# Values of the tile two back ahead of the transposes of the tile one back, in both attentions of an encoder layer

## The chip, the cores and the metric

The kernel runs on one core of one Trainium2 chip. The metric is the device time of one execution in microseconds (us); the time before is the median of three runs. A profile of one further execution shows what each engine did and when.

The engines have the names of the profile: PE is TensorE (matmuls; PEld is its loading of weights), DVE is VectorE, ACT is ScalarE, POOL is GpSimd, SP is the queue that issues most of the DMAs. PE writes only to PSUM, which has eight banks of 128 x 512 fp32 here; DVE and ACT read PSUM and copy to SBUF. Each engine works through its own queue in order.

## The reference

One encoder layer on two sequences (1024 and 256 rows of 1024 channels): a norm, one input projection, two attentions side by side, their gated sum, an output projection, and an MLP.

```python
def _layer(x, ...):
    h = _rmsnorm(x, g_mix)
    z = h @ w_in                       # qa, ka, va | qb, kb, vb | two gates
    gates = sigmoid(z[..., o6:] + b_gate)
    o_a, _ = _banded_attention(qa, ka, va, A_WINDOW, 1, rel_bias[:, :A_HEADS], sink)
    o_b = _dilated_mixture(qb, kb, vb, rel_bias[:, A_HEADS:])
    merged = gates[:, :, 0] * (o_a @ w_branch_a) + gates[:, :, 1] * (o_b @ w_branch_b)
    x = x + merged @ w_out
    h = _rmsnorm(x, g_mlp)
    return x + jnp.square(jax.nn.relu(h @ w_up)) @ w_down
```

Attention a has 8 heads in a window of 128 with a sink term in the denominator. Attention b has 12 heads in three groups of four, with dilations 1, 4 and 16; the three groups' outputs are merged by the softmax of their log-sums. In both, for a tile of 128 queries: scores = q k, plus a relative bias, minus the row maximum, exponential, row sum, and probabilities times values, divided by the sum.

## The kernel before

**Attention of one tile, in three steps.** Both attentions treat a tile of 128 queries and two heads at a time.

- scores: per head, PE multiplies q by k into a PSUM bank "sc" (two banks); DVE adds the bias and takes the row maximum in one instruction (L518 in attention b, L1027 in a), then negates the maxima (L521, L1031); ACT takes the exponential with the row sum (L523, L1033).
- transposes: PE turns the 128 x 128 blocks of probabilities (L534, L1048) into a bank "pt" (two banks, four blocks each), and copy() moves them to SBUF as the tile pt. A tile of b has two or four blocks, one of a four or six, so that six blocks need two banks.
- values: PE multiplies pt by v into the one bank "pv" (L546, L1062), copy() moves the result to SBUF as o, and POOL's queue stores o to DRAM.

copy() (L262, L264) gives its work to ACT and DVE in turn, in the order in which the program is written: the first call goes to ACT, the second to DVE, and so on.

**Attention b** runs beside the last five pairs of the input projection (about 355 to 590 us). All engines issue there in the order in which the program is written. attention_b() is a generator with three steps per tile, in the order scores(j), transposes(j - 1), values_of(j - 2) with load_v(j + 1). The projection calls tick() eighteen times per pair of columns, after each half of a group of matmuls (6 matmuls of 512 columns, or 12 of 256), and tick() takes two or three of these steps at a time: so many that the 188 steps are spread evenly over the calls. Between the calls stand the projection's own instructions: ACT copies or splits (a split is a copy rounded to the high part on ACT, "whi", and the subtraction of it on DVE, "wlo", L309 and L311), DVE sums, and once per pair four subtractions of 128 x 512 on POOL (L384 to L387), which combine the next pair's weights.

**Attention a** (about 598 to 755 us) has 40 tiles: 4 pairs of heads by 10 tiles of rows. A loop of 42 rounds runs, in round i, scores of tile i, transposes of tile i - 1 and values of tile i - 2. Between the steps tick(n) takes chunks of eight matmuls of logits() (five remaining gate columns, 31 chunks spread over 120 calls) and steps of the merge of attention b's groups. Up to round 35 a planner orders the instructions: it takes, for each engine, the earliest written instruction that it reckons to be ready. From round 36 on, through the sums of the sink and the division (sums_a, divide), the order of every engine is again that of the program. In rounds 36 to 39 turn_merged(i - 36) transposes the merged output of b into a bank "pt", ACT makes its high part, and low_b(i - 36) makes the low part on DVE, which frees the bank.

**The weights of what follows.** prepare() splits the next entry of a list of weights: five gate columns, then two pieces of w_branch_b, then four of w_branch_a, and so on. If its raw data has not been fetched, prepare() issues the load itself. weight(ahead) hands out the next entry, and splits entries until `ahead` more than that are ready: one more within logits(), none in the branches. Two raw loads, for the two pieces of w_branch_b, are issued at tick 96 and tick 104.

```python
def prepare(shared=False):
    i = len(ready)
    while len(raws) <= i:
        fetch()
    ...
def weight(ahead=None):
    i = taken[0]
    taken[0] += 1
    while len(ready) < min(len(specs), i + 1 + (AHEAD if ahead is None else ahead)):
        prepare()
    return ready[i]
```

**Behind the loop** sums_a() adds the sink to the denominators (DVE, an exponential on ACT, DVE), divide(t) divides the rows of attention a, open_gate() takes the sigmoids on ACT, the rest of the logits runs, and then the branches' products start, the first of them beside turn_a(0), which transposes the divided rows (L1194).

Of the kernel before, what the change touches and what calls it, by code (L numbers as in the profile page):

```python
# [97 lines left out]
def encoder_kernel(  # L98
# [125 lines left out]
# [5 lines that stand above are left out]
        _, shape, make = specs[i]  # L229
        hi, lo = make("whi", shape, F32R), make("wlo", shape, F32R)  # L230
        nc.scalar.activation(hi, raws[i], AF.Copy)
        h = shape[1] // 2 if shared else shape[1]
        for eng, k in ((nc.vector, slice(0, h)), (nc.gpsimd, slice(h, shape[1]))):
            if k.start < k.stop:
                eng.tensor_tensor(lo[:, k], raws[i][:, k], hi[:, k].bitcast(F32), op=ALU.subtract)
        ready.append((hi, lo))
# [240 lines left out]
    def attention_b(make):  # L477

        order = [(g, i, t, tile) for i in range(2) for g in (2, 1, 0) for t, tile in enumerate(_group_tiles(g))]
        n = len(order)  # L480
        held, live, bias = {}, {}, {}

        def load(j):

            if j >= n:
                return
            g, i, t, (pieces, W, _) = order[j]
            qk = held[j] = [make("qk", (P, 3 * P), n=3), None]
            for a, (p0, m, qa, ka) in enumerate(pieces):
                nc.sync.dma_start(qk[0][:, p0 : p0 + m], scr_qb[g][i][:, qa : qa + m])  # L490
                nc.sync.dma_start(qk[0][:, P + P * a : P + P * a + W], scr_kb[g][i][:, ka : ka + W])
            if t == 0:
                bias[g, i] = load_bias_b(g, i, make)

        def load_v(j):
            if j >= n:
                return
            g, i, t, (pieces, W, _) = order[j]
            v = held[j][1] = make("v", (P, 2, P), n=4)
            for a, (_, _, _, ka) in enumerate(pieces):  # L500
                for k in range(W // P):
                    nc.sync.dma_start(v[:, a + k, :], values_rows(g, i, ka // P + k))

        def scores(j):
            g, i, t, (pieces, W, c0) = order[j]
            qk, _ = held[j]
            whole, *flat = bias[g, i]
            b = whole[:, :, c0 : c0 + W] if c0 is not None else flat[pieces[0][2] >= NS]
            s = make("s", (P, 2, 2 * P), n=2)
            m = small.tile([P, 2], F32, name="m", tag="m")  # L510
            o = make("o", (P, ROW), n=6)
            for h in range(2):
                ps = bank("sc")
                rows = HALVES[h]
                for a, (p0, nq, _, _) in enumerate(pieces):
                    nc.tensor.matmul(ps[p0 : p0 + nq, :W], qk[rows, p0 : p0 + nq],
                                     qk[rows, P + P * a : P + P * a + W], start=True, stop=True)
                nc.vector.tensor_tensor_reduce(s[:, h, :W], ps[:, :W], b[:, h, :], 1.0, -3.0e38,  # L518
                                               op0=ALU.add, op1=ALU.max, accum_out=m[:, h : h + 1])
            nm, l = o[:, 2 * HD : 2 * HD + 2], o[:, 2 * HD + 2 :]  # L520
            nc.vector.tensor_scalar(nm, m, -1.0, None, op0=ALU.mult)  # L521
            for h in range(2):
                nc.scalar.activation(s[:, h, :W], s[:, h, :W], AF.Exp, bias=nm[:, h : h + 1],  # L523
                                     accum_out=l[:, h : h + 1])
            live[j] = s, o

        def transposes(j):
            W = order[j][3][1]
            s, o = live[j]
            pt = make("pt", (P, 4, P), n=2)  # L530
            ps = bank("pt")
            jobs = [(k, h) for k in range(W // P) for h in range(2)]
            for a, (k, h) in enumerate(jobs):
                nc.tensor.transpose(ps[:, P * a : P * a + P], s[:, h, P * k : P * k + P], ident)  # L534
            a = len(jobs)
            copy(pt[:, :a, :], ps[:, : P * a].rearrange("p (i q) -> p i q", q=P))
            live[j] = pt, o

        def values_of(j):
            g, i, t, (pieces, W, _) = order[j]  # L540
            (pt, o), (_, v) = live.pop(j), held.pop(j)
            pv = bank("pv")
            for h in range(2):
                for a, (p0, nq, _, _) in enumerate(pieces):
                    for k in range(W // P):
                        nc.tensor.matmul(pv[p0 : p0 + nq, HD * h : HD * h + HD], pt[:, 2 * k + h, p0 : p0 + nq],  # L546
                                         v[:, a + k, HALVES[h]], start=k == 0, stop=k == W // P - 1)
            copy(o[:, : 2 * HD], pv[:, : 2 * HD])
            for p0, nq, qa, _ in pieces:
                nc.gpsimd.dma_start(scr_b[g][qa : qa + nq, i, :], o[p0 : p0 + nq, :])  # L550

        load(0)
        load_v(0)
        yield
        load(1)
        yield
        for j in range(n + 2):
            if j < n:
                load(j + 2)
                scores(j)  # L560
            yield
            if 0 <= j - 1 < n:
                transposes(j - 1)
            yield
            if 0 <= j - 2 < n:
                values_of(j - 2)
            load_v(j + 1)
            yield

    def entering():  # L570
# [431 lines left out]
    if True:  # L1002
# [35 lines left out]
        def transposes(u, t):  # L1038
            W = tiles[t][1]
            s = live[u, t]  # L1040
            pt = a3("pt", (P, 6, P), 2)
            jobs = [(b, h) for b in range(W // P) for h in range(2)]
            banks = []
            for i, (b, h) in enumerate(jobs):
                if i % 4 == 0:
                    banks.append((i, min(len(jobs), i + 4), bank("pt")))
                ps = banks[-1][2]
                nc.tensor.transpose(ps[:, P * (i % 4) : P * (i % 4) + P], s[:, h, P * b : P * b + P], ident)  # L1048
            for i, e, ps in banks:
                copy(pt[:, i:e, :], ps[:, : P * (e - i)].rearrange("p (i q) -> p i q", q=P))  # L1050
            live[u, t] = pt
# [97 lines left out]
    if True:  # L1149
# [5 lines left out]
        def turn_merged(t):  # L1155

            if t in (0, 4, 8):
                ob_hi.block(t // 4)
                ob_lo.block(t // 4)
            ps = bank("pt")  # L1160
            for j in range(2):
                nc.tensor.transpose(ps[:, P * j : P * j + P], merged[t // 4][:, t % 4, P * j : P * j + P], ident)
            k = 8 if t < 8 else 2
            parts = []
            for j in range(2):
                hi, lo = (x.at(j, P * t, P).rearrange("p (q m) -> p q m", m=k) for x in (ob_hi, ob_lo))
                parts.append((hi, lo, ps[:, P * j : P * j + P].rearrange("p (m q) -> p q m", m=k)))
            banks_t["b", t] = parts
            for hi, _, src in parts:
                nc.scalar.activation(hi, src, AF.Copy)  # L1170
# [39 lines left out]
        order = [(u, t) for u in range(4) for t in range(NT)]  # L1210
        fill = logits()
# [17 lines left out]
        for i in range(len(order) + 2):  # L1229
            if i == 36:  # L1230

                last.enter_context(tc.manual_schedule(engines=ALL))
            if 36 <= i < 40:
                turn_merged(i - 36)
            if i in (38, 40):
                prepare()
            if i < len(order):
                u, t = order[i]
                if t == 0 and u < 3:
                    units[u + 1] = load_unit(u + 1), load_bias(u + 1, lambda name, shape: a3(name, shape, 2))  # L1240
                scores(u, t)
                tick(3 * i)
            else:
                next(fill)
            if 36 <= i < 40:
                low_b(i - 36)
            if 0 <= i - 1 < len(order):
                transposes(*order[i - 1])
                tick(3 * i + 1)
            if i >= len(order):  # L1250
                next(fill)
            if 0 <= i - 2 < len(order):
                values_of(*order[i - 2])
                tick(3 * i + 2)
            if i in (38, 39):
                load_o(i - 38)
        run(merges)
# [45 lines left out]
        for i, (x, b, c) in enumerate(jobs):  # L1303
            t0, n = BLOCKS[b]
# [503 lines left out]
```

## Time and profile before

| what | value |
|---|---|
| median of 3 runs | 1775.78 us (1774.84 to 1782.72) |
| the profiled execution | 1774.43 us |
| its span, from the first instruction to the last | 1772.7 us |
| stage of attention b | about 355 to 590 us |
| stage of attention a | about 598 to 755 us |
| branches' products | about 755 to 860 us |

The page of the profile gives each engine's busy time, its share of the span and its count of instructions; the views that are quoted below give the same for a stretch, or a group of instructions by line, or single instructions in order of time. In a row of the timeline the first number is the start in us from the beginning of the span, the second the length, then engine, line, operation and tiles (out<-in), the count where equal instructions were merged, and in brackets the idle time of the engine just before, with what ended it. In a row of the groups the numbers after the bar are the total busy time in us, the mean length in ns, and the idle time before. A row of the waits gives the total in us, how often, and the longest.

### The profile page before, as it was taken

How to read it: one execution, taken by the hardware profiler on the slowest of the kernel's cores; microseconds unless marked ns; L12 is line 12 of the kernel's file. 1: busy time of each engine (PE TensorE's matmuls, PEld its weight loads, DVE VectorE, ACT ScalarE, POOL GpSimd, SP SyncE). 2: the span in 40 equal slices, each digit the busy share in tenths (PEclk: the TensorE clock that was granted, in tenths of full speed). 3: DMA queues.
4: the chain of work that ended last, by engine and by line, in shares of the span. 5: the costliest groups of instructions: out<-in, count | busy, mean ns of one | idle time of the engine just before them, and what ended most of it. 6: DMA issues, size and time to landing. Idle time of an engine off the chain costs nothing.

```text
span 1772.7 us, 25231 instructions
## 1 busy us (share of the span) xinstructions
PE 1722.8 (97%) x9248; PEld 1461.3 (82%) x9248; DVE 990.1 (56%) x1683; ACT 711.5 (40%) x1531; POOL 550.5 (31%) x472
## 2 busy tenths in 40 slices
PE   7999999999999999999999899999999999999998
PEld 6898888877777899888888688888888788888886
DVE  6623323445545477576648645545454886667575
ACT  6232233344443355464336433333333433333345
POOL 0222321223322365100010355546555451305040
PEclk9999999999999999999999899999999999999999
DMA  6415335555464953185302134443345854633333
GB/s 232 146 38 164 105 112 142 138 164 151 138 169 130 286 144 97 63 273 190 132 36 99 64 126 129 152 151 117 118 146 201 296 191 149 227 101 118 120 113 119
DMA packets 214780, 256.36 MB, mean 145 GB/s; under 512 B 24887, under 2 KB 144523, under 8 KB 214528
## 3 DMA queue, kind: packets, MB, share of 16 engines
q1 hardware_dynamic: 201424, 228.26, 39.9%
q0 software_dynamic: 12144, 24.38, 4.5%
q10 hardware_dynamic: 1088, 2.10, 0.3%
q8 instruction: 73, 1.20, 0.3%
q14 instruction: 51, 0.42, 0.1%
HBM read 169.10 MB, written 90.73 MB: 147 GB/s over the span
## 4 chain that ended last, share of the span: by engine, by line
PE 60%; DVE 3%; ACT 2%; issue 1%; DMA 1%; POOL 0%; SPq 0%; ACTq 0%; DVEq 0%
PE dn L344 20%; PE mm L192 13%; PE x L344 10%; PE pv L344 5%; PE z L344 5%; PE pv L1062 2%; PE y L344 2%; PE pt L1048 1%; PE sc L1025 1%; DMA raw<-in_w_in_dram 1%; PE sc L1026 1%; DVE clo L311 1%; DVE ulo L186 0%; DVE v L1674 0%; DMA scr_g<-z 0%
## 5 line engine op out<-in xcount | busy, mean ns | idle before, releaser
L384 POOL TENSOR_TENSOR tb<-raw 128x512 f32<-128x512 f32 x30 | 39.8, 1326 | 450.0 <-PE mm L192 134.0
L344 PE MATMUL x<-chi,wlo 128*128 128x512 f32 x424 | 170.6, 402 | 7.5 <-ACT phi L185 7.3
L344 PE MATMUL dn<-dhi,ulo 128*128 128x512 f32 x448 | 174.6, 390 | 3.0 <-DVE ulo L186 3.0
L344 PE MATMUL dn<-dlo,uhi 128*128 128x512 f32 x448 | 174.3, 389 | 0.0
L344 PE MATMUL dn<-dhi,uhi 128*128 128x512 f32 x448 | 174.3, 389 | 0.0
L344 PE MATMUL x<-clo,whi 128*128 128x512 f32 x424 | 167.6, 395 | 0.1
L344 PE MATMUL x<-chi,whi 128*128 128x512 f32 x424 | 166.9, 394 | 0.0
L311 DVE TENSOR_TENSOR wlo<-ta,whi 128x1024 fp32r<-128x1024 f32 x30 | 56.6, 1888 | 187.8 <-ACT whi L309 187.8
L311 DVE TENSOR_TENSOR wlo<-raw,whi 128x1024 fp32r<-128x1024 f32 x60 | 93.9, 1564 | 103.7 <-ACT whi L309 103.7
L344 PEld LDWEIGHTS dn<-dhi,ulo 128*128 128x128 f32 x448 | 84.1, 188 | 21.3 <-DVE ulo L186 4.1
L344 PEld LDWEIGHTS x<-chi,wlo 128*128 128x128 f32 x424 | 81.0, 191 | 25.0 <-ACT phi L185 7.7
L186 DVE TENSOR_TENSOR ulo<-uraw,uhi 128x1024 fp32r<-128x1024 f32 x56 | 95.0, 1716 | 11.7 <-ACT uhi L185 11.7
L344 PEld LDWEIGHTS dn<-dlo,uhi 128*128 128x128 f32 x448 | 84.1, 188 | 17.5
L344 PEld LDWEIGHTS dn<-dhi,uhi 128*128 128x128 f32 x448 | 84.1, 188 | 17.4
L344 PEld LDWEIGHTS x<-chi,whi 128*128 128x128 f32 x424 | 80.8, 190 | 17.6
L523 ACT ACTIVATE s<-s,o 128x128 f32<-128x128 f32 (+1 forms) x120 | 52.4, 437 | 103.7 <-issue 58.3
L344 PEld LDWEIGHTS x<-clo,whi 128*128 128x128 f32 x424 | 81.0, 191 | 14.7 <-DVE clo L311 0.4
L1523 POOL TENSOR_TENSOR t<-raw,t 128x1024 f32<-128x1024 f32 x16 | 46.0, 2898 | 142.8 <-DMA raw<-in_w_down_dram 142.8
L1674 DVE TENSOR_TENSOR v<-v,dn 128x512 f32<-128x512 f32 x90 | 59.5, 682 | 43.2 <-PE dn L344 38.9
L344 PE MATMUL dn<-dhi,up 128*128 128x512 f32 x224 | 73.5, 389 | 0.0
L344 PE MATMUL pv<-phi,wlo 128*128 128x256 f32 x256 | 72.5, 283 | 0.9 <-ACT u L1694 0.9
L344 PE MATMUL pv<-plo,whi 128*128 128x256 f32 x256 | 72.6, 283 | 0.0
(332 smaller groups left out, 4785.9 us busy)
## 6 DMA issues: line engine op xcount, KB each, us to landing
scr_u<-u SPq DMA_DIRECT2D x112, 320.0 KB, 2.6
uraw<-scr_u SPq DMA_DIRECT2D x56, 512.0 KB, 4.2
raw<-in_w_in_dram SPq DMA_DIRECT2D x33, 512.0 KB, 5.4
raw<-in_w_up_dram SPq DMA_DIRECT2D x32, 512.0 KB, 5.5
raw<-in_w_down_dram SPq DMA_DIRECT2D x28, 512.0 KB, 6.4
sg<-scr_g SPq DMA_DIRECT2D x32, 256.0 KB, 5.2
uraw<-scr_u SPq DMA_DIRECT2D x28, 256.0 KB, 4.4
v<-scr_v SPq DMA_DIRECT2D x96, 64.0 KB, 2.2
```

The costliest lines, as they stand in the source:

```text
L186: nc.vector.tensor_tensor(lo, src, hi.bitcast(F32), op=ALU.subtract)
L192: nc.tensor.matmul(ps, a, b, start=i == 0, stop=i == len(seq) - 1)
L311: nc.vector.tensor_tensor(lo, src, hi.bitcast(F32), op=ALU.subtract)
L344: nc.tensor.matmul(ps, a, b, start=first and i == 0, stop=last and i == len(seq) - 1, skip_group_check=True)
L384: nc.gpsimd.tensor_tensor(tb[:, 0], b12, b11, op=ALU.subtract)
L523: nc.scalar.activation(s[:, h, :W], s[:, h, :W], AF.Exp, bias=nm[:, h : h + 1], accum_out=l[:, h : h + 1])
L1025: nc.tensor.matmul(ps[:, :W], q, st["k"][1][:, P * lo : P * lo + W], start=True, stop=False)
L1026: nc.tensor.matmul(ps[:, :W], q, st["k"][0][:, P * lo : P * lo + W], start=False, stop=True)
L1048: nc.tensor.transpose(ps[:, P * (i % 4) : P * (i % 4) + P], s[:, h, P * b : P * b + P], ident)
L1062: nc.tensor.matmul(pv[:, HD * h : HD * h + HD], pt[:, 2 * b + h, :], src, start=b == 0, stop=b == W // P - 1)
L1523: nc.gpsimd.tensor_tensor(o, a, b, op=ALU.subtract)
L1674: nc.vector.tensor_tensor(v, v, ps, op=ALU.add)
```

## The change

In attention b values_of(j - 2) and load_v(j + 1) stand ahead of transposes(j - 1). In attention a the values of tile i - 2 stand ahead of the transposes of tile i - 1, with the two calls of tick() exchanged accordingly. In the rounds from 36 on turn_merged() moves from the head of the round to behind the values, low_b() from ahead of the transposes to behind them, the extra chunk of logits of rounds 40 and 41 from behind the transposes to ahead of them, and the two calls of prepare() from the heads of rounds 38 and 40 to the ends of rounds 40 and 41.

```diff
@@ -559,12 +559,12 @@
                 load(j + 2)
                 scores(j)
             yield
-            if 0 <= j - 1 < n:
-                transposes(j - 1)
-            yield
             if 0 <= j - 2 < n:
                 values_of(j - 2)
             load_v(j + 1)
+            yield
+            if 0 <= j - 1 < n:
+                transposes(j - 1)
             yield
@@ -1230,10 +1230,6 @@
             if i == 36:
                 last.enter_context(tc.manual_schedule(engines=ALL))
-            if 36 <= i < 40:
-                turn_merged(i - 36)
-            if i in (38, 40):
-                prepare()
             if i < len(order):
                 u, t = order[i]
                 if t == 0 and u < 3:
@@ -1242,16 +1238,20 @@
                 tick(3 * i)
             else:
                 next(fill)
+            if 0 <= i - 2 < len(order):
+                values_of(*order[i - 2])
+                tick(3 * i + 1)
+            if 36 <= i < 40:
+                turn_merged(i - 36)
+            if i >= len(order):
+                next(fill)
+            if 0 <= i - 1 < len(order):
+                transposes(*order[i - 1])
+                tick(3 * i + 2)
             if 36 <= i < 40:
                 low_b(i - 36)
-            if 0 <= i - 1 < len(order):
-                transposes(*order[i - 1])
-                tick(3 * i + 1)
             if i >= len(order):
-                next(fill)
-            if 0 <= i - 2 < len(order):
-                values_of(*order[i - 2])
-                tick(3 * i + 2)
+                prepare()
             if i in (38, 39):
                 load_o(i - 38)
         run(merges)
```

## The prediction, made before the result was known

> **What bounds the kernel now.** I read the page first, then the stretches of the two attentions by window, then who waited for whom on TensorE there.
>
> ```profile
> span 1772.7 us, 25231 instructions
> ...
> PE 1722.8 (97%) x9248; PEld 1461.3 (82%) x9248; DVE 990.1 (56%) x1683; ACT 711.5 (40%) x1531; POOL 550.5 (31%) x472
> ```
> TensorE is busy for 97% of the span, so the change can only take away or add waits of TensorE. In the windows view the columns are length, then busy time of PE, PEld, DVE, ACT, POOL, then the granted clock:
>
> ```profile
> 355.00:590.00 235.00, 221.82 (x1465) 176.18 (x1465) 117.14 (x393) 101.05 (x347) 68.10 (x99) 0.98 0.55 160
> ...
> 598.00:726.00 128.00, 126.19 (x907) 117.68 (x905) 89.50 (x354) 68.66 (x210) 62.18 (x101) 1.00 0.51 139
> 726.00:755.00 29.00, 25.07 (x176) 22.61 (x175) 12.12 (x40) 10.96 (x36) 3.23 (x6) 1.00 0.17 54
> 755.00:806.00 51.00, 50.87 (x253) 41.79 (x252) 36.15 (x71) 31.53 (x70) 0.54 (x1) 1.00 0.77 260
> ```
> Attention b (355 to 590) has 13.2 us of idle TensorE and a clock of 0.98, which is another 235 x 0.02 = 4.7 us. Attention a has 1.8 us in the part that the planner orders and 3.9 us in its last rounds, whose order is by hand. Together some 24 us, 1.3% of the span: that is all that could be won. The waits, for 355 to 590 and then for 590 to 870 (total, times, longest):
>
> ```profile
> PE pt L534 <- ACT s L523: 7.3, 8, 2.0
> PE pv L546 <- issue: 2.5, 2, 2.3
> PE sc L516 <- DVE m L518: 2.4, 2, 2.2
> ```
> ```profile
> PE pt L1048 <- DVE oblo L1174: 2.0, 2, 1.1
> PE pt L1162 <- DVE oblo L1174: 1.9, 1, 1.9
> PE pt L1048 <- ACT s L1033: 1.5, 2, 1.4
> ```
> The largest, transposes (L534) behind exponentials (L523), is what one step more ahead of the transposes would relieve. Where does it come from?
>
> ```profile
> 375.00 3.07 DVE L521 TENSOR_SCALAR o<-m 128x2 f32<-128x2 f32 x1
> ```
> ```profile
> 426.62 3.40 DVE L521 TENSOR_SCALAR o<-m 128x2 f32<-128x2 f32 x1
> ...
> 430.10 0.51 ACT L523 ACTIVATE s<-s,o 128x256 f32<-128x256 f32 x1 [4.75 <-DVE o L521]
> ...
> 430.75 0.14 PEld L534 LDWEIGHTS pt<-ident,s 128*128 128x128 f32 x1 [0.86 <-ACT s L523]
> ```
> ```profile
> 481.90 4.71 DVE L311 TENSOR_TENSOR wlo<-raw,whi 128x1024 fp32r<-128x1024 f32 x1 [0.79 <-ACT whi L309]
> ```
> ```profile
> L386 POOL TENSOR_TENSOR ta<-raw,tb 128x512 f32<-128x512 f32 x4 | 5.1, 1268 | 0.0
> ```
> ```profile
> 359.46 0.71 PE L534 MATMUL pt<-ident,s 128*128 128x128 f32 x2 [1.16 <-ACT s L523]
> ...
> 571.45 0.71 PE L534 MATMUL pt<-ident,s 128*128 128x128 f32 x2 [0.59 <-ACT s L523]
> ```
> Mostly not from a queue that is one step too short: a two-element instruction of DVE lasts 3.07 or 3.40 us, and a subtraction 4.71, where they fall on POOL's four subtractions (L384 to L387, some 1.3 us each), once in each of four weight pairs. The three waits sum to 12.2 us; 1.2 is the first tile's and 0.6 the last one's (the two rows above), and the other 10.4 lie at these four places.
>
> **The change part by part.** It adds and removes no arithmetic in the loops.
>
> *a. Values ahead of transposes in attention b.* In old order the steps are scores(j), transposes(j-1), values(j-2); in new order scores(j), values(j-2), transposes(j-1). Transposes stand 5 steps behind their scores instead of 4; values only 2 behind their transposes instead of 4, with one scores step between. Counting the rule in tick() through (2 or 3 steps per tick, six to twelve matmuls between ticks), 11 ticks hold transposes(j), scores(j+2), values(j) together. There the copy of the transposes out of PSUM is exposed. And copy() alternates engines in program order: before, the first copy goes to ACT and then all pt copies to DVE and the o copies to ACT; with values first, the pt copies all go to ACT, behind the exponentials of the next tile, and the o copies to DVE.
>
> ```profile
> L264 DVE COPY pt<-pt 128x512 f32<-128x512 f32 x24 | 16.4, 685 | 5.2 <-PE pt L534 5.2
> ```
> ```profile
> L262 ACT ACTIVATE pt<-pt 128x512 f32<-128x512 f32 x18 | 10.6, 591 | 18.4 <-PE pt L1048 18.4
> ...
> L262 ACT ACTIVATE pt<-pt 128x256 f32<-128x256 f32 x13 | 5.0, 382 | 9.1 <-PE pt L1048 8.9
> ```
> ```profile
> 441.58 0.70 PE L516 MATMUL sc<-qk 64*128 64x256 f32 x4
> 442.22 0.66 PE L534 MATMUL pt<-ident,s 128*128 128x128 f32 x4
> 442.63 0.36 PE L344 MATMUL mm<-phi,wlo 128*128 128x256 f32 x1
> ```
> Four transposes end 0.66 after their start, the copy takes 0.59, and from the exponential's end (430.61) to TensorE's next start (430.75) pass 0.14: 1.39. TensorE arrives after 0.41 of transposes and 0.64 of scores: 1.05. So 0.34 of waiting; two transposes with the 0.38 copy give 0.1 to 0.4. I take 0.35 x 11 = 3.9 less 1.0 for the three that lie in the blocks of b, and 1.6 for ACT's other work in the queue ahead (a 0.59 copy before five of them, a 1.05 split near two): **+4.5** (1.4 if ACT is always free, 9 if a split is always ahead). load_v moves forward with the values; SP's queue keeps its order and issues nothing more, and no row of the waits above names v.
>
> *b. The four POOL blocks.* POOL's subtractions are neither removed nor shortened. Transposes now have a step more, but the values step inherits the old distance: its copy on ACT stands behind the exponentials of the tile whose scores came 3 steps before, just where the transposes stood. In the block at 482:
>
> ```profile
> 486.87 0.69 PE L516 MATMUL sc<-qk 64*128 64x128 f32 x4 [2.19 <-DVE m L518]
> ...
> 488.24 0.39 ACT L523 ACTIVATE s<-s,o 128x128 f32<-128x128 f32 x1
> ```
> The scores still wait until 486.87. The transposes needed only the first exponential, which had ended when the second began, and could go on at 488.38; the values need both (488.63) and the copy of 0.38 and 0.14: 489.15, 0.8 later. A block that has six more matmuls ahead of its wait gains up to 1.5 instead. POOL's start also moves: it stands in POOL's queue behind the store of o, and that behind the o copy, now on DVE. For the four I take **+2.0** (from -6, a chunk of matmuls won in each, to +3.6). The clock:
>
> ```profile
> 489.00:492.00 3.00, 3.00 (x11) 2.43 (x10) 0.59 (x4) 0.88 (x4) 0.56 (x1) 0.50 0.64 180
> ```
> After such a wait TensorE runs some 3 us at half clock, 1.5 us lost; the stage's 4.7 us of clock are three such spells. I leave these as they are.
> The Trainium skill ("TensorE: Matmul & The Clock Gate", What's actually happening) gives the low clock only after an idle window of about 3.4 us; here waits of about 2 us brought it, so the trace disagrees. By the page only the wait in f could halve the clock.
>
> *c. The ends.* The first tile's scores and transposes shared a tick and lost 1.2 us; now its values wait some 0.7. The last tile but one has transposes and values in one tick with no scores between. **+0.5**.
>
> *d. Attention a, planner's part.* The same shortness, 0.3 us a tile in 34 rounds, where no logits matmuls lie between (about half): 5 us, but the planner may draw logits matmuls in. **+2.0** (0 to 8). There is nothing to win but the 1.5 at its first tile, which nothing moves.
>
> *e. Last rounds, by hand.* The 3.9 us of waits for oblo and behind the weight split go. But six transposes need two PSUM banks and the turned merge has one of the two: the last two wait for the first copy, 0.66 + 0.69 + 0.14 - 0.41 = 1.1 in round 36, and about 1.4 in round 37 where the copy falls to ACT behind exponentials. **-1.4** (-3.9 to 0).
>
> *f. The split weights.* ready counts decide here. Without prepare() at round 38, weight() for the last logits column, at round 39, itself splits the first weight of branch b, since it keeps one ahead. Then prepare() at rounds 40 and 41 splits the second weight of b and the **first of branch a**, which has not been fetched: the load is issued on the spot, and ACT and DVE, in order, stand behind it with the sink sums, the division and the sigmoids.
>
> ```profile
> 739.18 1.06 ACT L231 ACTIVATE whi<-raw 128x1024 fp32r<-128x1024 f32 x1
> ...
> 740.28 1.23 DVE L235 TENSOR_TENSOR wlo<-raw,whi 128x1024 fp32r<-128x1024 f32 x1 [3.26 <-ACT whi L231]
> ```
> ```profile
> 754.99 0.26 ACT L1072 ACTIVATE nm_a<-nm_a 128x80 f32<-128x80 f32 x1
> ...
> 755.28 0.24 DVE L1073 TENSOR_TENSOR l_a<-l_a,nm_a 128x80 f32<-128x80 f32 x1 [3.27 <-ACT nm_a L1072]
> ...
> 755.56 0.65 DVE L1074 RECIPROCAL l_a<-l_a 128x80 f32<-128x80 f32 x1
> ...
> 756.25 1.29 DVE L1185 TENSOR_TENSOR o<-o,l_a 128x512 f32<-128x512 f32 x2
> ```
> ```profile
> raw<-in_w_branch_b_dram SPq DMA_DIRECT2D x2, 512.0 KB, 4.2
> ```
> ```profile
> raw<-in_w_branch_a_dram SPq DMA_DIRECT2D x4, 512.0 KB, 6.7
> ```
> ```profile
> 750.97 1.00 PE L1062 MATMUL pv<-vp,pt 128*128 128x64 f32 x8
> ```
> ```profile
> 751.97 1.97 PE mm L192 x16
> ...
> 754.78 6.48 PE mm L192 x32
> ```
> From the end of the last transposes: copy 0.59, split 1.06 and 1.23, logits copy 0.69, then the load 4.2, split 1.06 and 1.23, two sums of 0.24, exponential 0.26, reciprocal 0.65, division 0.65, and 0.4 of hand-overs: 12.5 us. TensorE has 1.97 + 6.48 and 1.00 of values, 9.4, before it transposes the divided rows. It waits 3.1, or 5.6 at a landing of 6.7; the planner can put the first product's six matmuls (6 x 0.20 = 1.2) ahead; half clock behind it would cost 1.5. **+3.2**, near the wait itself (0 if the planner and a faster load cover it, 5.6 + 1.5 = 7.1).
>
> Sum: 4.5 + 2.0 + 0.5 + 2.0 - 1.4 + 3.2 = +10.8. The profiled execution took 1774.43 (span 1772.7 and 1.7 around it), 1.35 below the median 1775.78: **1785 us**.
>
> **The rivals.** *Covered* (the change moves waits and does little): DVE and ACT are half idle in attention b, the planner hides d, the load of f lands early. Then a 2, b -1, c 0.5, d 0, e -1.4, f 1: 1774.43 + 1.1, about 1776. For it: 23 of 24 us idle have causes that stay. Against: f is in the program's order, not in a guess.
> *Faster*: POOL's subtractions start some 2 us later against DVE's instructions in two blocks, since their queue now waits for DVE's o copy. If DVE's subtraction gets in first each time, POOL stands behind it, off the path: the 10.4 us and the 4.7 us of clock go, less a and f partly: 1774.4 - 15 + 5 = 1764. It decides when DVE's instruction starts ahead of POOL's first. Against: two of the four keep their order.
> The Trainium skill ("SBUF — State Buffer", Who interferes with whom) says just that: issue order decides, and the second of the two is blocked until the first ends. Rows 426.62 and 481.90 agree for POOL first; none here shows DVE first.
>
> **How the numbers follow.** Forecast 0.50, covered 0.38, faster 0.12. The bound of 0.5% is 8.9 us, about what a measurement of this kernel can tell from no change: slower 0.50, same 0.38, faster 0.12. The forecast's own range is 1782 to 1796; with covered the range is 1770 to 1796, and the faster case and sums with d and f at their upper ends stay outside.
>
> **What would show it.** Right: pt copies on ACT and o copies on DVE in attention b; waits of values (L546) for ACT's copy, some eleven of 0.2 to 0.6; a DMA row of the branch a weight issued near 754, ahead of the gates, and a TensorE wait of 2 to 5 us at L1194 or just after; the oblo waits gone. Wrong: no TensorE gap between 755 and 770, or DVE's long rows gone from attention b. A planner that reorders attention a wholesale would upset d.

## The result, and the profile after

The changed kernel takes **1787.12 us** (median of 8 runs, 1783.5 to 1791.86), the kernel before 1776.53 (8 runs beside it, 1774.26 to 1782.72). The ratio is **1.0056**, 95% interval 1.0037 to 1.0075: slower by 10 us, where 1785 was forecast. The profiled execution has a span that is 11.8 us longer than before's 1772.7. The page:

```profile
span 1784.5 us, 25293 instructions
...
PE 1730.2 (97%) x9248; PEld 1462.7 (82%) x9248; DVE 977.4 (55%) x1683; ACT 723.7 (41%) x1531; POOL 550.8 (31%) x472
```

TensorE has the same 9248 matmuls and is busy 7.4 us longer, so more than half of the loss is not idle time but slower matmuls. DVE gave 12.7 us of work up and ACT took 12.2 more: the copies of transposes went over to ACT, as forecast. The windows view of attention b, from its first scores to the first scores of attention a, first the changed kernel (with a stretch of 6 us in it), then the kernel before. The columns are length, busy time of PE, PEld, DVE, ACT and POOL, the granted clock, DMA share and GB/s:

```profile
355.60:605.73 250.13, 235.02 (x1513) 184.19 (x1513) 104.10 (x393) 113.65 (x348) 75.38 (x108) 0.96 0.57 162
489.00:495.00 6.00, 4.70 (x16) 3.62 (x16) 1.69 (x9) 2.41 (x10) 2.53 (x4) 0.55 0.44 126
```
```profile
355.18:598.38 243.20, 230.18 (x1512) 183.58 (x1513) 116.96 (x393) 101.05 (x347) 73.56 (x108) 0.98 0.57 167
```

The stage grew by 6.9 us, of which idle TensorE is 2.1 (15.1 against 13.0), and the clock fell from 0.98 to 0.96. Half clock stands here for the stretches in which the granted clock drops to about half, as in the second row; its cost is the length of a stretch times one less its granted clock. Added up in windows of 1 us, it was 10.3 us here and 5.1 before. The waits of TensorE in the changed kernel, for 355 to 595 and for 595 to 880 (total, times, longest):

```profile
PE sc L516 <- DVE m L518: 5.9, 3, 2.5
PE pv L546 <- ACT pt L262: 5.9, 8, 1.6
PE pv L546 <- issue: 2.4, 1, 2.4
```
```profile
PE pt L1194 <- DVE oblo L1174: 2.9, 1, 2.9
...
PE pt L1194 <- DVE o L1185: 2.0, 1, 2.0
```

Transposes no longer wait for exponentials. Values wait for ACT's copy instead, and scores for DVE's maxima. Behind attention a there are two new waits at the transposes of the divided rows. This table holds the stages of the profiles, each from the start of one matmul to the start of the next one named, and for the first stage the idle time of TensorE and the cost of half clock in it; the kernels e1 to e4 and e8 are described below.

| us | before | after | e1 | e2 | e3 | e4 | e8 |
|---|---|---|---|---|---|---|---|
| first scores of b to first scores of a | 243.20 | 250.13 | 246.37 | 244.43 | 244.80 | 244.37 | 246.45 |
| idle TensorE in it | 13.0 | 15.1 | 14.8 | 12.1 | 15.2 | 12.1 | 14.7 |
| half clock in it | 5.1 | 10.3 | 6.8 | 8.5 | 5.1 | 8.5 | 6.8 |
| to the first transposes of divided rows | 162.71 | 165.51 | 163.86 | 164.04 | 163.56 | 163.19 | 161.37 |
| to the last transposes of divided rows | 44.53 | 49.32 | 44.38 | 49.33 | 45.98 | 45.64 | 46.23 |
| to the first matmul of the output projection | 46.25 | 44.63 | 46.26 | 44.63 | 46.25 | 44.63 | 44.63 |

### The profile page after: what moved, and what is told of

It reads as the page before. It is cut to its first block, busy times and chain, and to the rows that moved or that the text cites. A ratio compares the mean times of both kernels' runs of the same rounds, so it can differ in the third digit from the quotient of the medians.

```text
span 1784.5 us, 25293 instructions
## 1 busy us (share of the span) xinstructions
PE 1730.2 (97%) x9248; PEld 1462.7 (82%) x9248; DVE 977.4 (55%) x1683; ACT 723.7 (41%) x1531; POOL 550.8 (31%) x472
## 4 chain that ended last, share of the span: by engine, by line
PE 58%; DVE 4%; ACT 3%; DMA 2%; issue 2%; POOL 0%; SPq 0%; ACTq 0%; DVEq 0%; POOLq 0%
PE dn L344 20%; PE mm L192 12%; PE x L344 9%; PE pv L344 5%; PE z L344 4%; PE pv L1062 2%; PE y L344 2%; PE pt L1048 1%; PE sc L1025 1%; PE sc L1026 1%; DMA raw<-in_w_in_dram 1%; DVE clo L311 1%; DVE ulo L186 0%; DMA scr_u<-u 0%; DVE v L1674 0%
## 5 line engine op out<-in xcount | busy, mean ns | idle before, releaser
L311 DVE TENSOR_TENSOR wlo<-raw,whi 128x1024 fp32r<-128x1024 f32 x60 | 100.1, 1668 | 105.6 <-ACT whi L309 104.7
L344 PEld LDWEIGHTS dn<-dhi,uhi 128*128 128x128 f32 x448 | 84.1, 188 | 17.6
L344 PEld LDWEIGHTS dn<-dlo,uhi 128*128 128x128 f32 x448 | 84.1, 188 | 17.3
L344 PEld LDWEIGHTS x<-chi,whi 128*128 128x128 f32 x424 | 81.2, 191 | 17.6
L344 PEld LDWEIGHTS x<-clo,whi 128*128 128x128 f32 x424 | 81.5, 192 | 14.8 <-DVE clo L311 0.4
L344 PE MATMUL z<-chi,wlo 128*128 128x512 f32 x184 | 72.5, 394 | 0.0
```

Source lines behind the costliest of these rows:

```text
L311: nc.vector.tensor_tensor(lo, src, hi.bitcast(F32), op=ALU.subtract)
L344: nc.tensor.matmul(ps, a, b, start=first and i == 0, stop=last and i == len(seq) - 1, skip_group_check=True)
```

## The experiments

All are ratios to the kernel before, run beside each on the same chip. The groups e1 to e4, e5 to e8 and e9 to e12 ran on three different chips, so kernels of different groups are compared by their ratios. A ratio of 0.001 is 1.8 us.

### First four: which part of the change costs

**e1, attention b's order alone.** The edit is the first half of the diff shown above, and attention a is as before.

> Attention b's values ahead of its transposes, and nothing else of the change. Theory: the changed kernel's loss has two sources that add, one in attention b (its stage is 6.9 us longer, +7.35 at the first scores of a against +0.42 at the first scores of b) and one behind attention a; so this kernel takes 1776.5 + 7 = 1783 to 1784 us, and the first scores of a stand at 604 to 607 against 598.4. Rival one: all of the loss comes from the weight that is split early, and attention b's longer stage is chance of that profile: 1775 to 1778. Rival two: the two parts work on each other (a stretch in b shifts a into a worse place): 1784 to 1788 here too, with a loss behind 755 although a is as before.

Measured: 1779.32 us, 1.0016 (1.0001 to 1.0032), or 2.8 us, with 0.2 to 5.7 possible. That is well under the theory's 7 and a little above rival one. The window from 355 to 590, whose row for the kernel before stands in the prediction (221.82 busy), and the waits in it:

```profile
355.00:590.00 235.00, 220.05 (x1442) 171.44 (x1441) 104.76 (x394) 112.70 (x346) 68.95 (x98) 0.97 0.56 155
```
```profile
PE sc L516 <- DVE m L518: 5.9, 3, 2.5
PE pv L546 <- ACT pt L262: 5.4, 8, 1.6
PE pv L546 <- issue: 2.3, 1, 2.3
```

The three waits are close to those of the changed kernel (5.9, 5.4 and 2.3 against 5.9, 5.9 and 2.4), so the idle time is the program's doing: 14.95 us against 13.18 in this window, that is 1.8 more. The half clock is not: it cost 6.8 us in this profile and 10.3 in the changed kernel's, for the same instructions up to there.

**e2, attention a's part alone**, with all that belongs to it; attention b as before.

> Attention a's part of the change with attention b as before, the third weight split included. Theory: attention a itself gains about 1, the third split costs about 6.6, and 1.3 comes back at the output projection: 1776.5 + 4 to 5 = 1780 to 1782, with the wait at the first transposes of the divided rows (L1194) of 2 us or more twice. Rival one, the loss is all of this part: 1786 to 1788. Rival two, the loss is all in attention b: 1775 to 1777.

Measured: 1782.82 us, 1.0034 (1.0021 to 1.0046), 6 us. The theory's 4 to 5 was a little too low, and both rivals fall. The two waits at L1194 are there (1.84 and 3.03), and so is the table's 49.33.

**e3, the change without the third split:**

```diff
-            if i >= len(order):
+            if i == len(order):
                 prepare()
```

> The changed kernel without its third weight split ahead of the sums of the sink: prepare() at the end of round 40 alone, so that w_b's two pieces are split there and the first piece of w_branch_a where it was before. Theory: ACT and DVE no longer stand behind a load of the weight, the wait at the first transposes of the divided rows goes, and with it the second one and two stretches of half clock: 1787.1 - 6 to 7 = 1780 to 1781; the first transposes of the divided rows stand 5 to 6 us nearer to the last values of a. Rival: the wait there comes from the division and the gates all the same (the order of the last rounds, or the later sums), and nothing changes: 1786 to 1788.

Measured: 1781.79 us, 1.0018 (1.0005 to 1.0031), which is 0.0038 or 6.7 us under the changed kernel's 1.0056. That difference of two ratios is good to about 4 us either way (estimated from their two intervals). The median lies just above the 1780 to 1781 of the theory. The transposes of the divided rows in time, with no wait at either:

```profile
764.93 0.60 PE L1194 MATMUL pt<-ident,o 128*128 128x128 f32 x4
...
766.76 0.60 PE L1194 MATMUL pt<-ident,o 128*128 128x128 f32 x4
```

So the third split is the larger part of the loss. What is left of attention a's part is the difference to e1: 0.0002, or 0.4 us, nothing that can be told from zero.

**e4, the third split alone, in the old order:**

```diff
+            if i == 41:
+                prepare()
             if i in (38, 39):
                 load_o(i - 38)
```

> The kernel before with one edit: prepare() a third time, at the end of round 41. It splits the first piece of w_branch_a ahead of the sums of the sink, and issues its load on the spot; no order of steps is changed. Theory: this alone costs what the changed kernel loses behind attention a, 5 to 7 us: 1781 to 1783. My recorded term for it was 3.2: 1779.7. Rival: alone it is hidden (before's last rounds end with the second split at round 40 rather than 41, so that ACT and DVE are free earlier): 1776 to 1778.

Measured: 1777.93 us, 1.0009 (0.9996 to 1.0021), or 1.6 us, with -0.7 to 3.7 possible. The rival is right: alone, the split costs little or nothing. Why, the rows of e4 show (SP's issue of the load, ACT's split, TensorE's first transposes of divided rows):

```profile
754.17 0.32 SPq L1085 DMA_DIRECT2D scr_g<-gs  x1
...
754.54 0.43 SPq L222 DMA_DIRECT2D raw<-in_w_branch_a_dram  x1
...
758.64 1.06 ACT L231 ACTIVATE whi<-raw 128x1024 fp32r<-128x1024 f32 x1 [1.27 <-DMA raw<-in_w_branch_a_dram]
...
763.60 0.60 PE L1194 MATMUL pt<-ident,o 128*128 128x128 f32 x4
```

Against those of the changed kernel:

```profile
760.29 1.23 DVE L235 TENSOR_TENSOR wlo<-raw,whi 128x1024 fp32r<-128x1024 f32 x1 [3.63 <-ACT whi L231]
...
761.43 0.68 DVE L264 COPY gs<-mm 128x512 f32<-128x512 f32 x1
...
762.14 0.32 SPq L1085 DMA_DIRECT2D scr_g<-gs  x1
...
762.55 0.39 SPq L222 DMA_DIRECT2D raw<-in_w_branch_a_dram  x1
...
766.73 1.06 ACT L231 ACTIVATE whi<-raw 128x1024 fp32r<-128x1024 f32 x1 [5.94 <-DMA raw<-in_w_branch_a_dram]
...
768.97 0.23 DVE L1071 TENSOR_TENSOR nm_a<-nm_a,nsink 128x80 f32<-128x80 f32 x1
...
770.50 1.29 DVE L1185 TENSOR_TENSOR o<-o,l_a 128x512 f32<-128x512 f32 x2
...
771.24 1.32 PE L1194 MATMUL pt<-ident,o 128*128 128x128 f32 x8 [1.99 <-DVE o L1185]
...
780.20 0.69 DVE L1185 TENSOR_TENSOR o<-o,l_a 128x512 f32<-128x512 f32 x1 [3.35 <-DMA o<-scr_o]
...
782.78 0.76 PE L1194 MATMUL pt<-ident,o 128*128 128x128 f32 x4 [2.90 <-DVE oblo L1174]
```

The load stands in SP's queue behind the store of a block of logits (L1085), and that behind their copy. In the changed kernel the copy stands on DVE behind the second split, so the load leaves 2.4 us after TensorE's last values of attention a began (760.19). In e4 it leaves 2.2 us before them (756.78). Those 4.6 us are what covers the chain there: load, split, sums, division.

### The next four: where the time in attention b is, and the load

**e5 and e6, POOL's subtractions apart, in the kernel before.** In both, the four subtractions of each of the last pairs come one at a time between groups of matmuls, behind the split of the raw columns; in e5 on DVE, in e6 still on POOL. The edit is that of e5; in e6 eng is nc.gpsimd, and the last two lines stand in three places.

```diff
-        if late:
+        if late or apart:
             yield from part(raw[0], (P, KC, P))
...
-        nc.gpsimd.tensor_tensor(tb[:, 0], b12, b11, op=ALU.subtract)
-        nc.gpsimd.tensor_tensor(ta[:, 1], b22, b12, op=ALU.subtract)
...
+        eng = nc.vector if apart else nc.gpsimd
+        eng.tensor_tensor(tb[:, 0], b12, b11, op=ALU.subtract)
+        if apart:
+            yield
+        eng.tensor_tensor(ta[:, 1], b22, b12, op=ALU.subtract)
+        if apart:
+            yield
...
             one.store()
             beside()
+            if late:
+                next(nb, None)
```

> The kernel before, with the four subtractions of each of the last pairs (L384 to L387) on DVE instead of POOL, one at a time between groups of matmuls, and behind the split of the raw columns instead of ahead of it. Theory: the four blocks of attention b (10.4 us of waits, and the half clock behind them, 5.1 in that profile) come from DVE's instructions standing behind POOL's four; without them the waits and most of the half clock go, for 16 more DVE instructions of some 0.6 us each that lie beside matmuls: 1777 - 9 to 15 = 1762 to 1768, and no DVE instruction of two elements over 0.5 us in attention b. Rival: the waits come from the load on ACT and DVE as such; four more subtractions on DVE bring other waits: 1774 to 1779.

> As the run beside it, with the subtractions apart from each other in the same places, but still on POOL. Theory: one subtraction of 1.3 us holds DVE up to 1.3 us instead of 3 to 4.7, which two score banks and the queue mostly cover: 1777 - 5 to 10 = 1767 to 1772. Rival one: DVE is held as long in all, only in more places, and each of the sixteen costs PE a wait: 1774 to 1780. Rival two: POOL alone has nothing to do with it (the split of raw columns on ACT and DVE in the same step is the cause): it is moved too here, so DVE and POOL give the same time.

Measured: e5 1759.73 us, **0.9894** (0.9871 to 0.9917); e6 1760.77 us, 0.9906 (0.9882 to 0.9929). Both took off 17 to 19 us, more than either expectation. The largest wait of TensorE left in attention b and DVE's two-element instructions there (groups: total, mean in ns), for e5:

```profile
PE pt L541 <- ACT s L530: 1.3, 2, 0.8
```
```profile
L528 DVE TENSOR_SCALAR o<-m 128x2 f32<-128x2 f32 x60 | 10.3, 171 | 2.1
```

and for e6 (groups, then shortest, median and longest in ns):

```profile
L528 DVE TENSOR_SCALAR o<-m 128x2 f32<-128x2 f32 x60 | 18.5, 309 | 2.2
```
```profile
L528 DVE TENSOR_SCALAR o<-m x60: 168/169/1602, 357.1 to 555.7; 128x2 f32<-128x2 f32 x60
```

and for the kernel before (groups):

```profile
L521 DVE TENSOR_SCALAR o<-m 128x2 f32<-128x2 f32 x60 | 20.0, 333 | 2.2
```

In e6 these instructions lose 8.2 us against e5 (18.5 less 10.3), nearly the 9.7 of the kernel before, but never more than 1.4 at once, and TensorE is idle no longer in attention b's stage than in e5 (3.6 us against 3.5). Rival one of e6 is right about DVE and wrong about TensorE.

**e9, the split ahead, the four subtractions together**, separates the two edits of e6. Its edit is that of e6 without the `yield`s between the subtractions and without the calls of next().

> The kernel before with the split of the raw columns ahead of POOL's four subtractions, as in the two kernels with subtractions apart, but the four issued together as before. It tells which of their two edits took the 17 us away. Theory (four subtractions in a row hold DVE's short instructions for 3 to 4.7 us): the split escapes, what DVE has next behind it is held instead, and most of the loss stays: 1772 to 1779, with a two-element instruction of DVE (L521 of before) of 3 us or more in at least two of the four places. Rival (the split in the same step was the cause, and its place is the cure): 1758 to 1764.

Measured: 1778.29 us, 1.0011 (0.9998 to 1.0024). The whole 17 us are back. One of the four places, in time:

```profile
375.65 1.30 POOL L385 TENSOR_TENSOR tb<-raw 128x512 f32<-128x512 f32 x1
...
376.37 3.05 DVE L522 TENSOR_SCALAR o<-m 128x2 f32<-128x2 f32 x1
...
379.46 1.27 POOL L388 TENSOR_TENSOR tb<-raw,ta 128x512 f32<-128x512 f32 x1
```

So it is the row of subtractions that costs, not the split's place: a two-element instruction of 0.17 lasts 3.05 behind it. The same happens in two more of the four places (3.40 and 3.17); in the other one a split's subtraction lasts 4.71. The theory is right.

**e7, the copies exchanged.** Attention b's new order as in e1, but copies of transposes on DVE and those of o on ACT, as before the change.

```diff
                     att_b = attention_b(stage)
+                    flip[0] ^= 1
...
     first_part.close()
+    flip[0] ^= 1
```

> Attention b's values ahead of its transposes (as in the first run), with copy()'s turn exchanged at the start of attention b and back at its end, so that the copies of transposes go to DVE and those of o to ACT as in the kernel before. Theory of the recorded terms: the exposed pt copy on ACT, behind exponentials, makes most of what attention b's stage loses net of half clock (238.1, 235.9 and 235.9 in three profiles of the old order, 239.9, 239.6 and 239.7 in the new): on DVE it stands behind less, and 1.5 to 3 of the 3.1 us go: 1776 to 1778, stage net of half clock 236.5 to 238. Rival: the distance alone counts (two steps between transposes and values, whoever copies), and POOL's subtractions now hold pt copies too: 1779 to 1782, stage net of half clock 240 or more.

Measured: **1799.35 us**, 1.0110 (1.0088 to 1.0132), 17 us above e1 by the ratios. My theory had the sign wrong, and the rival was too small by far. The waits, and the first large one in time:

```profile
PE pv L546 <- issue: 19.5, 11, 5.7
```
```profile
375.46 1.04 ACT L309 ACTIVATE whi<-raw 128x1024 fp32r<-128x1024 f32 x1
...
376.54 4.66 DVE L311 TENSOR_TENSOR wlo<-raw,whi 128x1024 fp32r<-128x1024 f32 x1 [2.19 <-ACT whi L309]
...
380.19 2.14 POOL L387 TENSOR_TENSOR tb<-raw,ta 128x512 f32<-128x512 f32 x1
...
381.12 0.41 DVE L264 COPY pt<-pt 128x256 f32<-128x256 f32 x1
...
381.63 1.08 PE L546 MATMUL pv<-v,pt 128*128 128x64 f32 x4 [5.60 <-issue]
```

The releaser is given as "issue", but the rows show it: values start 0.1 after the copy of transposes has ended on DVE (381.53). That copy stands behind the low part of a split, which first waited for its high part on ACT and was then held by POOL.

**e11, the same with the subtractions on DVE, apart**, asks whether POOL is all of it.

> Values ahead of transposes in attention b, copies of transposes on DVE and of o on ACT (the kernel that took 1799), with the subtractions on DVE, apart. Theory: those 20 us came from copies of transposes that stood in DVE's queue behind a split held by POOL (5.6 us of TensorE's wait at 381.6, 4.1 at 438.9), so that without POOL's subtractions they go: 1760 to 1765. Rival: copies of transposes on DVE are late by themselves (behind the sums and the splits' low parts, 0.3 to 0.6 each, in 36 tiles), and 16 more subtractions make it worse: 1770 to 1785.

Measured: 1776.18 us, 0.9993 (0.9979 to 1.0007), against e5's 0.9894: 18 us above it. The rival is right: without POOL the copies of transposes on DVE are late all the same. The kernel that differs from this one in attention b by the exchange of the copies alone is e10, below: its stage from the first scores of b to the first scores of a takes 231.55 us, here it takes 242.55.

```profile
PE pv L553 <- issue: 10.5, 11, 2.8
```
```profile
375.18 1.04 ACT L309 ACTIVATE whi<-raw 128x1024 fp32r<-128x1024 f32 x1
...
376.25 1.23 DVE L311 TENSOR_TENSOR wlo<-raw,whi 128x1024 fp32r<-128x1024 f32 x1 [2.19 <-ACT whi L309]
...
377.40 0.69 DVE L385 TENSOR_TENSOR tb<-raw 128x512 f32<-128x512 f32 x1
...
378.00 0.42 DVE L264 COPY pt<-pt 128x256 f32<-128x256 f32 x1
...
378.52 0.63 PE L553 MATMUL pv<-v,pt 128*128 128x64 f32 x4 [2.76 <-issue]
```

Here the copy on DVE stands behind both halves of a split (ACT's, then DVE's) and a subtraction; a copy on ACT would stand behind the first half alone. With two steps between transposes and values that shows as 2.76 us of wait.

**e10, the changed kernel with the subtractions on DVE, apart.**

> The changed kernel with the subtractions of the last pairs on DVE, apart. It shows what the change costs where no block of POOL is left. Theory: the third split's 5.3 us stays (it lies behind attention a), attention b's own loss falls from about 3 us to the 1 to 2 of its short steady waits: 1759.7 + 6 to 8 = 1766 to 1768, still slower than the kernel before with the same edit. Rival one: without the blocks the new order is the better one in attention b, 1760 to 1764. Rival two: the copies of transposes on ACT wait more now that more splits of ACT come close: above 1769.

Measured: 1770.09 us, 0.9966 (0.9953 to 0.9978). That is 13 us above e5 by the ratios (10 by the medians), so the change costs no less where the blocks are gone. The windows view of the stage of attention b, e10 and then e5, and the largest group of waits in e10:

```profile
355.20:586.75 231.55, 224.81 (x1512) 177.24 (x1513) 100.70 (x409) 113.37 (x347) 52.76 (x92) 1.00 0.61 175
```
```profile
355.90:585.21 229.31, 225.81 (x1513) 180.77 (x1514) 113.20 (x409) 101.53 (x348) 52.59 (x92) 0.99 0.62 177
```
```profile
PE pv L553 <- ACT pt L262: 4.4, 7, 1.6
```

TensorE is idle for 6.7 us against 3.5, so the new order adds 3.2 us of idle time with no block of POOL left. The longest wait is the last tile's. By the stages of the table, e10 stands against e5 with 231.55 to 229.31, 166.08 to 163.43, 49.85 to 45.20 and 44.64 to 46.25: 7.9 us longer in all, of which the stretch to the last transposes of the divided rows, the third split's, is the largest part. Rival two's number came true, but its reason covers only 4.4 us.

**e8, the third load issued early, in the changed kernel:**

```diff
-            if n in (96, 104):
+            if n in (96, 104, 112):
                 fetch()
```

> The changed kernel with one edit: a third raw load, for the first piece of w_branch_a, is issued at tick 112 beside those of ticks 96 and 104, so that the third split finds its data. Theory: it is the load issued on the spot, behind the store of the logits that waits for their copy (762.1 to 766.7 in the changed kernel's profile), that ACT, DVE and the division stand behind; with the data there the gates and the division come 4.2 us earlier and both waits at L1194 go, while the 1.6 us that the ready weight gives back ahead of the output projection stay: 1787.1 - 5 to 7 = 1780 to 1782, at or below the kernel without the third split. Rival one: the split itself (1.06 + 1.23) or SP's later loads keep the wait: 1784 to 1787. Rival two: the early load waits for its buffer in SP's queue and holds up the rest there: above 1787.

Measured: 1778.18 us, 1.0006 (0.9991 to 1.0020): 0.0050 or 9 us off the changed kernel, more than expected.

```profile
757.41 1.05 ACT L231 ACTIVATE whi<-raw 128x1024 fp32r<-128x1024 f32 x1
...
761.43 1.29 DVE L1185 TENSOR_TENSOR o<-o,l_a 128x512 f32<-128x512 f32 x2
...
764.48 0.60 PE L1194 MATMUL pt<-ident,o 128*128 128x128 f32 x4
```

ACT goes from the second split (755.94) to the third with a wait of 0.25 for a copy, the division ends before TensorE asks for it, both waits at L1194 are gone (one of 1.9 at L192, for DVE's L1327, came), and the 44.63 of the table stays. So the load on the spot was the cost, not the split. Some of the 9 us may be chance: this profile had no half clock between 600 and 880, the changed kernel's had two stretches.

**e12, the kernel before with all that seemed good**: subtractions on DVE, apart; a third split at the end of round 41; its load at tick 112.

> The kernel before, its orders kept, with the subtractions on DVE apart, and the third split at the end of round 41 with its load issued at tick 112. Theory: the split finds its data and lies beside matmuls, and a ready first piece of w_branch_a takes 1.6 us away ahead of the output projection (44.63 instead of 46.25 us from the last transposes of the divided rows to it, in every kernel with the third split): 1759.7 - 1 to 2 = 1757.5 to 1759. Rival: DVE and ACT stand 2.3 us longer ahead of the division, which costs what the later stretch gives: 1759 to 1761.

Measured: 1760.72 us, 0.9909 (0.9894 to 0.9923), no better than e5, as the rival said. The 1.6 us ahead of the output projection came (44.63 against 46.25), but the stretch before it grew by 2.6 (47.84 against 45.20), 1.7 of it one stretch of half clock. **The best version is the kernel before with POOL's subtractions apart**, 1.1% faster than before and 1.6% faster than the changed kernel (e5, with e6 and e12 within the intervals).

## Why the prediction was right, point by point

The forecast was 1785 from +10.8; measured was a ratio that is 10 us. Step by step it splits into e1, the step from e1 to e3, and the step from e3 to the changed kernel: 2.8 + 0.4 + 6.7. By construction this adds up to the whole; e2 checks it from the other side, with 6.0 for the last two together.

Every run lists its granted clock, which splits its time in two: time x (1 - clock), the cost of half clock, and the rest. The means over all runs of each kernel, with the 35 runs of the kernel before beside e1 to e4 (standard errors up to 1.1 for half clock and 0.6 for the rest; in the other two groups the kernel before has 18.8 and 17.3 of half clock, 1759.5 and 1760.4 of the rest):

| us | before | e1 | e2 | e3 | e4 | after | e8 | e5 | e9 | e7 | e10 |
|---|---|---|---|---|---|---|---|---|---|---|---|
| half clock | 17.2 | 16.6 | 19.5 | 15.7 | 17.6 | 19.7 | 15.6 | 7.9 | 19.0 | 25.2 | 10.1 |
| the rest | 1760.6 | 1763.9 | 1763.9 | 1765.3 | 1760.8 | 1767.8 | 1763.8 | 1752.1 | 1760.2 | 1773.3 | 1760.5 |

- **a, b and c, attention b (+7.0 recorded): 2.8, with 0.2 to 5.7 possible.** The direction is right, the size is not. By the table e1's loss lies in the rest (3.3) and none that shows in half clock. Terms a and c were +4.5 and +0.5; where the blocks are gone, the new order adds 3.2 of idle time (e10 against e5). Term a counted eleven exposed copies; the changed kernel has eight such waits, 5.9 in all, of which 2.2 are the first and the last tile's (0.55 and 1.62). The other six come to 3.7, the longest 1.47, and e10 has a wait at the same tile for five of them (0.54, 0.35, 0.41, 0.76 and 0.60), so they are the order's own; the blocks lengthen one of them, 0.76 to 1.47. The reason given in a fails for the engine: "the pt copies all go to ACT, behind the exponentials" was written as a cost. e7 and e11 show that it is the cover: with copies on DVE, the same order costs 17 us more with POOL's blocks, and 11 in attention b's stage without them.
- **b, the four blocks (+2.0):** about nothing. POOL's rows still hold DVE, as forecast; in three of the four places they now hold a split's subtraction (4.18, 4.82 and 3.98 instead of 1.23), and the waits moved from transposes to scores and values. But the new order costs no more idle time with the blocks than without: 2.5 in the first table (14.9 in the mean of the four new orders, 12.4 in that of the three old ones) against 3.2. Rival "faster" fell: the blocks do not dissolve by themselves. e9 and e6 show what dissolves them.
- **The clock ("I leave these as they are"):** in the two profiles compared, half clock cost another 5.1 us, which looked like half of the loss. More profiles of the same stage show that this was chance: the means are 7.4 in the old order and 7.3 in the new (first table). The step stands for attention b.
- **d and e, attention a (+0.6 together):** 0.4, within what can be told from zero. The waits for oblo in the last rounds (3.9) went, as forecast, and three of 0.85, 0.83 and 0.56 came.
- **f, the split weights (+3.2, to 7.1 at most): 6.7.** The mechanism is the recorded one: load on the spot, ACT and DVE behind it, wait at L1194. The load took 4.2 as reckoned (762.55 to 766.73), and the first wait was 1.99 where 3.1 was forecast. Left out was what follows. The loads of o, behind it in SP's queue, left from 775.2 on (in e3 from 768.8), a later division waited 3.35 for one of them, and TensorE 2.9 for what stood behind that division on DVE. In e3 and e8 TensorE waits near this place too, at L192 for DVE's L1327, but only 1.6 and 1.9. Half clock is the other part: between e3 and the changed kernel it grows by about 4 in the table of the runs (standard error 1.3), between e3 and e2, on one chip, by as much, and the profile has two stretches that cost 3.4, where f's +3.2 held none. Something was missed on the other side: the ready weight takes 1.6 us away ahead of the output projection. This row of the kernel before is gone in the changed one:

```profile
851.87 0.50 PE L192 MATMUL mm<-whi,mlo 128*128 128x512 f32 x1 [1.31 <-DVE mlo L186]
```

"f is in the program's order, not in a guess" was the argument against rival "covered", and it held, but only for this order: e4 shows the same split nearly free.

The main causes were forecast rightly; that the total came out so close is partly luck: attention b was put too high by 4.2 and f too low by 3.5, and the two made up for each other. What stays open: f's size, which the intervals leave between about 3 and 11, and why one wait brings half clock and another does not.

## What to carry to other kernels

A step moved nearer to its consumer is priced by what stands ahead of its copy in program order on the copying engine, so before moving it, follow which engine an alternating helper will give it to: the parity was worth more here than the order. A prefetch placed earlier is cheap only if its load leaves early enough. Issued on the spot it stands behind the stores already in the same queue: in e4 these were early and the split was nearly free, in the changed kernel they were late and everything in order behind the load waited. And where a two-element instruction lasts 3 us, look at what runs beside it: breaking up POOL's rows of subtractions won more (17 to 19 us) than the change of order cost.

## What the runs showed of the hardware

**Half clock comes in equal pieces, and not with every wait.** In the attentions and branches of the profiles every stretch costs a multiple of about 1.7 us (1.7, 3.4 or 5.1), so that each piece is some 3.4 us at half clock. Waits of like length bring it or don't: in the changed kernel the waits of 2.35 at 431.9 and of 2.52 and 1.47 at 488 to 490 were followed by two and three pieces, one of 1.84 at 381.2 by none. In e5, waits of 0.6 and 0.8 at its first tile brought one; in e10, 2.46 at 592.3 none. The Trainium skill ("TensorE: Matmul & The Clock Gate", What's actually happening) has windows of 3.4 us that run freely; the size of the pieces agrees, and where a wait falls in such a window could be the chance seen here, which no run tests.

**POOL and DVE hold each other in both directions.** In e7 DVE's subtraction of a split at 376.54, which takes 1.23 in e11, takes 4.66: it is held while POOL's first subtraction runs (from 376.40), and also by the second and third, which start later than it does (377.63 and 378.85). POOL's fourth, which starts at 380.19, just when the split goes on, takes 2.14 instead of the third's 1.26. The prediction says that no row shows DVE ahead of POOL, but the kernel before has one: its split of 481.90 ends at 486.61, and POOL's fourth subtraction beside it, at 485.59, takes 2.14 too. The Trainium skill ("SBUF — State Buffer", Who interferes with whom) says that issue order decides who is blocked. POOL's first and fourth subtractions agree; the second and third, which hold a split that had started before them, do not.
